# The first block's gates, queries, keys and values by seven block products in place of eight, with the sums of the weights made on VectorE

## The chip, the cores and the metric

The kernel runs on one NeuronCore of a Trainium2 chip. The metric is the device time of one execution in microseconds (us). The kernel before took 1728.72 us in the median of three runs (1728.32 to 1729.15).

## The reference

A token sequence of 512 tokens with 2048 features goes through two blocks; all values are float32. The change touches only the first, which puts 16 meta tokens in front (528 rows) and computes:

```python
hn = rmsnorm(h, pre_norm_g[layer])
proj = jnp.einsum('bld,dc->blc', hn, w_in[layer])
qa, ka, va, ga, qb, kb, vb, gb = jnp.split(proj, SPLIT_POINTS, axis=-1)
ya = gqa_axial_mixer(qa, ka, va, ...) * jax.nn.silu(ga)
yb = diff_attn_mixer(qb, kb, vb, ...) * jax.nn.silu(gb)
y = jnp.einsum('blc,cd->bld', jnp.concatenate([ya, yb], axis=-1), w_out[layer])
h = h + rmsnorm(y, post_norm_g[layer])
```

Mixer A has 8 query heads of 128 features on 2 key heads, mixer B has 8 heads with two softmaxes each. `ga`, `gb`, `qb`, `kb` and `vb` have 1024 columns each: 8 units of 128. The second block (stick-breaking attention, a convolution and a recurrence, another two projections) is left as it is.

## The kernel before, in words

**Products.** Each float32 operand is split into two float32r halves: `split` (L147 to L149) rounds to a high half on ScalarE (L148) and subtracts it on VectorE for the low half (L149). A product is then three matmuls, high x high, high x low, low x high (`PASSES`). The activations `big` hold both halves of all 16 K tiles (128 features each) of x, scaled by the norm's gain, 528 columns. The factor of the norm's root (`rbc`, one value for each token) is put in when a result is taken from PSUM.

**Weights.** The weights are packed on the host in half units of 128 x 1024 (eight K tiles of 128 columns). `load_next` loads a half unit on the SP queue (L266) into one of three buffers `wraw` and splits it into one of three buffers `wsp`. `take` asks for a half unit and lets two more be loaded ahead (`AHEAD`).

**Order of the first block.** KA, VA, QA0, then the eight gate units GA, QA1, the eight gate units GB, and for each of eight heads B the units QB, KB, VB; then the output projection O1. A gate or QB unit is 16 K tiles x 3 passes = 48 matmuls of 512 columns (`fm_real`), a KB or VB unit 96 matmuls of 264 columns (`fm_all`, 528 in two halves). A unit's result lies in a `pj` buffer of two PSUM banks, of which there are two. For a gate, `silu2` multiplies by `rbq` on VectorE (L432), takes the tanh on ScalarE (L433) and combines on VectorE (L434) into `ybuf`, where the attention's result is later multiplied in (`gate_y`, L439; for B L732). `split_y` then splits a slot of `ybuf` into `big` as the operand of O1.

**Who runs when.** The order on TensorE is written by a planner at build time: `run` takes steps of the main stream (the projections) and, when their due time by a clock of planned TensorE time has come, steps of side streams (the attention of each head: scores, softmax, transposes, values). So the matmuls of the heads stand between those of the projections, and on VectorE, ScalarE and the SP queue the instructions of both are mixed. Each engine takes its own instructions in that written order.

Of the kernel before, what the change touches and what calls it, by code (L numbers as in the profile page):

```python
# [16 lines left out]
P = 128  # L17
# [4 lines left out]
NM = 16  # L22
# [18 lines left out]

def _units():
# [6 lines left out]
    for name, n in (("KA", 2), ("VA", 2), ("GA", 8), ("QB", 8), ("KB", 8), ("VB", 8), ("GB", 8)):  # L49
        for i in range(n):  # L50
            u[(name, i)] = ("fm", 0, i, cols)
            cols += P
# [23 lines left out]

def _sequence():
# [19 lines left out]
def hybrid_two_block_kernel(ctx: ExitStack, tc: tile.TileContext, wp, xT, xtok, par, lvec, cst, rg, pg, lruw, out):  # L97
# [34 lines left out]
    def et(n=L):  # L132
        return T([P, L], "e", F32, 5)[:, :n]
# [98 lines left out]
    ybuf = T([P, KT, NTOK], "ybuf")  # L232
    yflat = flat(ybuf)
# [12 lines left out]
    h1d = dram.tile([NTOK, D], F32, tag="h1d", name="h1d")  # L246

# [7 lines left out]
    loaded = []  # L255

    def load_next(n=1024):
# [4 lines left out]
        raw = T([P, 1024], "wraw", F32, 3)  # L262
        w = T([P, 2, 1024], "wsp", F32R, 3)
# [7 lines left out]
    taken = [0]  # L271

    def take(unit, h):
        i = taken[0]
        assert seq[i] == (unit, h), (seq[i], unit, h)
        taken[0] = i + 1
        while len(loaded) < min(len(seq), i + 1 + AHEAD):
            for _ in load_next():
                pass
        return loaded[i]  # L280

# [15 lines left out]
    def fm_two(units, ps, lag):  # L297

        w = [None, None]
        for i in range(KT + lag):  # L300
            for u, kt in ((0, i), (1, i - lag)):
                if 0 <= kt < KT:
                    if kt % 8 == 0:
                        w[u] = take(units[u], kt // 8)
# [9 lines left out]
    def fm_all(unit, ps, after_kt=None):  # L314
        return fm(unit, [(ps[:, 0, :HL], (0, HL)), (ps[:, 1, :HL], (HL, L))], after_kt)

# [3 lines left out]
    def tm(units, x0, evac, kgs=range(4), toks=range(NT), before_unit=None, after_unit=None, chore=None):  # L320
# [4 lines left out]
        for i, unit in enumerate(units):  # L325
# [5 lines left out]
            if last:  # L331
                ws_ = [take(unit, 0), take(unit, 1)]
# [80 lines left out]
    kvraw = [ar[:, i * L : (i + 1) * L] for i in range(4)]  # L413
# [7 lines left out]
    qs_, ks_, vs_ = ar[:, 4608:5120], ar[:, 5120:5648], ar[:, 2560:3088]  # L421
    osb, osq, orr = ar[:, 3088:3600], ar[:, 3600:4112], ar[:, 1824:2336]
# [18 lines left out]
    def split_y(s):  # L441
        split(big[:, 0, s, :NTOK], big[:, 1, s, :NTOK], ybuf[:, s, :])

# [36 lines left out]
    def pv_steps(h, tag, e, cols, vt, vs, use, extra=()):  # L480

        for hf in range(2):
            yield when("pt", "ptt", (tag, h, 2 * hf))
            hold("pt")
            pt = T([P, 2, 4, 256], "pt", F32R)
# [37 lines left out]
    def side_norms():  # L523
# [3 lines left out]
        for j in range(5):  # L527
# [3 lines left out]
            xs = yflat[:n, (j % 2) * 2048 : (j % 2) * 2048 + 2048]  # L531
            nc.sync.dma_start(xs, xtok[j * P : j * P + n, :])
            act.activation(yflat[:n, 4096:6144], xs, AF.Square, accum_out=ss0[:n, j : j + 1])
# [24 lines left out]
    def side_kv(g):  # L558
# [3 lines left out]
        kb, t1, u = (yflat[:, (3 * g + i) * 640 : (3 * g + i + 1) * 640] for i in range(3))  # L562
# [71 lines left out]
    def a_sums(h, e):  # L634
        g = h // 4
        yield when(("gate", h), ("va", g))
        yield from pv_steps(h, "ea", e, lambda j: slice(j * P, min(L, (j + 1) * P)), lambda: va[g][0], lambda: va[g][1], lambda hf, o: gate_y(h, hf, o))
        post(("y", h), 1500)
# [4 lines left out]
    def b_values(h, vt):  # L643
        yield when(("projv", h), "pss", *([("sumb", h - 2)] if h > 1 else [("suma",)]))
        vt[:] = v_tiles(vs_, h % 2)
# [60 lines left out]
    def b_sums(h, e, vt):  # L706
# [6 lines left out]
        yield from pv_steps(h, "eb", e, tile_cols, lambda: vt[0], lambda: vt[1], use, [("normed", h - 1)] if h else [])  # L713
# [17 lines left out]
        y = ybuf[:, 8 + h, :]  # L731
        dve.tensor_tensor(y, osb, y, ALU.mult)  # L732
        post(("normed", h))
        post(("y", 8 + h), 5000)


    yt = blocks(yflat, D)
# [193 lines left out]
    def main_work():  # L931
# [4 lines left out]
        for i in range(2):  # L936
            ps = pjt()
            yield from fm_all(("VA", i), ps)
            act.copy(halves(kvraw[2 + i]), ps[:, :, :HL])
            post(("kv", 2 + i), 1000)  # L940

        def qa(c):
            def evac(accs):
                yield when("rbc", *([("qaused", 0)] if c else [("va", 0), ("va", 1)]))
                for t in accs:
                    act.mul(qraw[:, t, :], accs[t], rnat[:, t : t + 1])

            yield from tm([(f"QA{c}", kg) for kg in range(4)], NM, evac)
            post(("qa", c), 1000)

        def gate(unit, slot):
            ps = pjt()
            yield from fm_real(unit, ps, NM)
            ins = silu2(ps[:, 0, :], rbq, ybuf[:, slot, :])
            post(("gate", slot), 2000)
            return ins

        yield from qa(0)
        for h in range(8):
            yield from gate(("GA", h), h)  # L960
        yield from qa(1)
        for h in range(8):
            ins = yield from gate(("GB", h), 8 + h)
        with tc.issue_after(ins):
            lnload[0] = act.preload_act_table_set("natural_log_exp_and_others").ins

        def split_ready(kt):
            if there(("y", kt)) and kt not in ysplit:
                ysplit.add(kt)
                split_y(kt)  # L970

        def spread(kt):
            if kt % 4 == 3:
                split_ready(kt // 4)

        ysplit = set()
        for h in range(8):
            ps = pjt()
            yield from fm_real(("QB", h), ps, NM)
            if h:  # L980
                yield when(("qkused", h - 1))
            dve.scalar_tensor_tensor(qs_, ps[:, 0, :], -0.125, rbq, op0=ALU.mult, op1=ALU.mult)
            ps = pjt()
            yield from fm_all(("KB", h), ps)
            dve.tensor_tensor(halves(ks_), ps[:, :, :HL], halves(rbc), ALU.mult)
            post(("projb", h))
            ps = pjt()
# [257 lines left out]
```

## Time and profile before

| what | value |
|---|---|
| median of the runs | 1728.72 us |
| profiled execution | 1727.61 us |
| its span | 1725.8 us |
| busy share of TensorE (PE) | 99% |
| busy share of VectorE (DVE) | 59% |
| busy share of ScalarE (ACT) | 45% |
| granted TensorE clock | 1.00 |
| HBM read, written | 175.89 MB, 8.39 MB |

A page names engines PE (matmuls), PEld (weight loads), DVE (VectorE), ACT (ScalarE), POOL (GpSimd) and SP (the queue that issues DMAs). A group row has the line in the kernel, engine, operation, what is written <- what is read, shapes and count; then busy us and mean ns of one; then the idle time of the engine just before them and what ended it. A row in order of time has start, length, engine, line and tiles; a row that ends in x92 merges 92 instructions. Matmuls overlap, so their pace is read from starts.

### The profile page before, as it was taken

The page shows a single profiled execution, that of the slowest core. Times are in us where ns is not written, and L with a number is a line of the kernel's source. Part 1 is how long each engine was busy: PE and PEld are TensorE (multiplying, and loading weights), DVE is VectorE, ACT ScalarE, POOL GpSimd, SP SyncE. Part 2 cuts the span into 40 slices and gives each one's busy share as a digit, 9 for nine tenths or more (in the row PEclk, how much of TensorE's full clock was granted, in tenths as well). Part 3 has the DMA queues.
Part 4 walks back from the last instruction along what each step waited for, and adds up shares of the span by engine and source line. Part 5 has one row for each costly group of instructions (what it writes and reads, how often), then busy time and mean ns, then how long its engine had stood idle before and what let it go on. Part 6 is the DMA issues. An engine that isn't in the chain of part 4 may idle for free.

```text
span 1725.8 us, 23791 instructions
## 1 busy us (share of the span) xinstructions
PE 1714.7 (99%) x9496; PEld 1477.6 (86%) x9496; DVE 1015.9 (59%) x1694; ACT 783.8 (45%) x1276; POOL 91.0 (5%) x85
## 2 busy tenths in 40 slices
PE   8999999999999999999999999999999999999998
PEld 8888888889999999988788998888888888888887
DVE  5748634864566666775557869743223664575433
ACT  6434423443445555564445547822223664575311
POOL 0100001100001101000000001100000000010000
PEclk9999999999999999999999999999999999999999
DMA  8321122222221222222567653222222212432223
GB/s 314 121 98 62 63 84 86 68 79 74 76 84 64 72 74 74 74 69 78 171 196 270 218 190 109 92 94 90 98 98 90 81 61 88 153 115 74 86 97 123
DMA packets 53854, 185.81 MB, mean 108 GB/s; under 512 B 6112, under 2 KB 7776, under 8 KB 52064
## 3 DMA queue, kind: packets, MB, share of 16 engines
q1 hardware_dynamic: 53744, 184.30, 32.2%
q8 instruction: 74, 1.21, 0.3%
q14 instruction: 36, 0.29, 0.1%
HBM read 175.89 MB, written 8.39 MB: 107 GB/s over the span
## 4 chain that ended last, share of the span: by engine, by line
PE 96%; DVE 2%; issue 0%; DMA 0%; POOL 0%; ACT 0%; SPq 0%; DVEq 0%; ACTq 0%; POOLq 0%
PE pj L181 84%; PE pmt L181 4%; PE pss L181 4%; PE ptt L184 2%; PE pmt L184 1%; PE bank L181 1%; PE pss L184 1%; DVE wsp L149 0%; DMA wraw<-in_wp 0%; POOL ybuf L450 0%; SPq L374 0%; ACT wsp L148 0%; POOL ar L450 0%; SPq L266 0%; DVE sm L574 0%
## 5 line engine op out<-in xcount | busy, mean ns | idle before, releaser
L181 PE MATMUL pj<-big,wsp 128*128 128x264 f32 (+2 forms) x4608 | 809.0, 332 | 5.9 <-ACT big L375 5.3
L181 PEld LDWEIGHTS pj<-big,wsp 128*128 128x128 f32 x4608 | 688.2, 189 | 86.9 <-ACT big L375 5.6
L181 PE MATMUL pj<-wsp,big 128*128 128x512 f32 x3072 | 736.5, 396 | 0.6 <-DVE big L149 0.6
L181 PEld LDWEIGHTS pj<-wsp,big 128*128 128x128 f32 x3072 | 569.6, 188 | 131.3 <-DVE big L149 0.9
L149 DVE TENSOR_TENSOR wsp<-wraw,wsp 128x1024 fp32r<-128x1024 f32 (+1 forms) x299 | 363.1, 1215 | 387.1 <-ACT wsp L148 386.7
L148 ACT CAST wsp<-wraw 128x1024 fp32r<-128x1024 f32 (+1 forms) x299 | 310.8, 1040 | 496.0 <-PE pj L181 391.6
L148 ACT CAST pt<-ptt 128x512 fp32r<-128x512 f32 (+2 forms) x96 | 50.3, 524 | 76.1 <-PE ptt L184 76.1
L687 ACT ACTIVATE e<-e,sm 128x528 f32<-128x528 f32 x64 | 47.2, 737 | 77.6 <-DVE sm L684 77.1
L149 DVE TENSOR_TENSOR pt<-ptt,pt 128x512 fp32r<-128x512 f32 (+2 forms) x96 | 59.4, 619 | 35.4 <-ACT pt L148 34.7
L181 PEld LDWEIGHTS pmt<-pt,vv 128*128 128x128 f32 x528 | 69.1, 190 | 3.6
L181 PE MATMUL pss<-kk,qq 128*128 128x264 f32 x448 | 71.4, 287 | 0.0
L181 PE MATMUL pmt<-pt,vv 128*128 128x256 f32 (+1 forms) x528 | 69.6, 280 | 0.0
L181 PEld LDWEIGHTS pss<-kk,qq 128*128 128x128 f32 x448 | 63.5, 188 | 3.7
L684 DVE CUSTOM_DVE_ANT_0 e<-pss,ar 128x528 f32<-128x528 f32 x64 | 45.0, 703 | 31.4 <-PE pss L181 30.9
L184 PE MATMUL ptt<-ident,e 128*128 128x128 f32 x336 | 52.6, 273 | 0.1
L184 PEld LDWEIGHTS ptt<-ident,e 128*128 128x128 f32 x336 | 40.6, 140 | 6.9 <-DVE e L627 0.5
L432 DVE TENSOR_TENSOR e<-pj,rbc 128x512 f32<-128x512 f32 x32 | 22.0, 688 | 39.7 <-PE pj L181 39.7
L885 POOL TENSOR_SCALAR_AFFINE_SELECT e<-e 128x128 f32<-128x128 f32 x32 | 15.7, 490 | 476.2 <-ACT e L884 471.1
L654 POOL TENSOR_SCALAR ar<-ar 128x912 f32<-128x912 f32 x8 | 23.4, 2930 | 211.9 <-DVE sm L684 207.4
L624 ACT ACTIVATE e<-pss,sm 128x528 f32<-128x528 f32 x32 | 22.4, 701 | 23.5 <-DVE sm L622 23.4
L450 POOL TENSOR_TENSOR ar<-ar 128x256 f32<-128x256 f32 x16 | 18.4, 1172 | 242.9 <-DVE ar L447 242.9
L894 ACT ACTIVATE e<-e 128x128 f32<-128x128 f32 (+3 forms) x32 | 15.0, 470 | 28.8 <-DVE e L893 28.5
(202 smaller groups left out, 1168.9 us busy)
## 6 DMA issues: line engine op xcount, KB each, us to landing
wraw<-in_wp SPq DMA_DIRECT2D x295, 512.0 KB, 3.5
e<-in_xT SPq DMA_DIRECT2D x16, 264.0 KB, 4.4
ybuf<-in_xtok SPq DMA_DIRECT2D x4, 1024.0 KB, 7.2
ar<-in_xtok SPq DMA_DIRECT2D x4, 1024.0 KB, 5.9
h1d<-ybuf SPq DMA_DIRECT2D x4, 1024.0 KB, 5.4
ybuf<-h1d SPq DMA_DIRECT2D x12, 256.0 KB, 3.6
out<-ybuf SPq DMA_DIRECT2D x12, 256.0 KB, 2.1
ar<-in_pg SPq DMA_DIRECT2D x1, 1024.0 KB, 4.8
```

Source lines behind the costliest of these rows:

```text
L148: act.copy(hi, src)
L149: dve.tensor_tensor(lo, src, f(hi), ALU.subtract)
L181: _queue(nc.tensor.matmul(out, lhsT, rhs, start=start, stop=stop).ins, cost)
L184: _queue(nc.tensor.transpose(out, in_, identity).ins, 110.0)
L432: dve.tensor_tensor(g, g_ps, rb, ALU.mult)
L450: pool.tensor_tensor(v4(blocks(u))[:, :, :, a, :], v4(x)[:, :, :, 1 - a, :], v4(blocks(s))[:, :, :, a, :], ALU.mult)
L624: act.activation(halves(x), sv, AF.Exp, bias=nm, accum_out=l[:, 0:1])
L654: pool.tensor_scalar(bias, dist, 2.0 ** (-(h + 1)), None, op0=ALU.mult)
L684: dve.tensor_tensor_reduce(out=halves(x), in0=s[:, :, :HL], in1=halves(bias[:, b0 : b0 + L]), scale=1.0, scalar=3e38, op0=ALU.add, op1=ALU ...
L687: act.activation(x, x, AF.Exp, scale=-1.0, bias=nm, accum_out=l[:, m : m + 1])
L885: pool.affine_select(z[:, t * P : w], z[:, t * P : w], [[-1, P]], ALU.is_gt, -1e30, base=0, channel_multiplier=1)
L894: act.activation(c, c, AF.Exp)
```

## The change

Units are taken in 20 pairs (`PAIRS`): two gates, QB with KB of a head, or VB of two heads. Over the first 12 K tiles the pair is a 2 x 2 block product: two halves of the K tiles (`KS` = 6 each), two halves of the tokens (264 each), two units. Seven block products with sums of blocks replace the eight. The last four K tiles (`NCL` = 4) are computed as before, and added in PSUM (`rest`).

- The sums of the blocks of x are made once, by `side_x`, from x loaded again, into `x23`, `x1s` and over a part of `big`.
- The sums of the blocks of the weights are made for each pair on VectorE, by `produce`: four additions of 128 x 768. Seven splits of 768 columns and two of 512 replace four of 1024. Raw weights and split weights lie in four slots each in the same memory as before.
- `seven` runs the products of a pair on four PSUM banks, and combines them in eight VectorE operations on 264 (or 248) columns.
- The memory of `ybuf` is taken by `x23` in this stage. The gates are written to HBM (`gated`) and fetched when a head needs them; a head's result goes to HBM (`yd`) and is fetched for its split (`fetch_y`). All of these stand on the SP queue.
- QA1 moves ahead of the gates, and its result goes through HBM (`qd`); VA1 moves behind it. The pool of `e` buffers has six in place of five. In the last half of a unit one half unit less is asked for ahead, in the whole kernel. Weights of O1 are not loaded before the last pair (`barred`).

```diff
-    seq = [("VA", 0), ("VA", 1)] + [("QA0", kg) for kg in range(4)]
-    seq += [("GA", i) for i in range(8)] + [("QA1", kg) for kg in range(4)] + [("GB", i) for i in range(8)]
-    for h in range(8):
-        seq += [("QB", h), ("KB", h), ("VB", h)]
+    seq = [("VA", 0)] + [("QA0", kg) for kg in range(4)] + [("QA1", kg) for kg in range(4)] + [("VA", 1)]
...
-        return T([P, L], "e", F32, 5)[:, :n]
+        return T([P, L], "e", F32, 6)[:, :n]
...
+    def load_raw(p, r, slot):
...
+        nc.sync.dma_start(raw, wq[p, r] if r < 4 else wc[p, r - 4])
+    def produce(p, i):
...
+        add = lambda a, b: dve.tensor_tensor(r(a), r(a), r(b), ALU.add)
...
+        n = NCL * P if i in (6, 8) else WS
+        if i == 2:
+            add(0, 1)
+        slot = at[place]
+        w = halves(wsp_all[:, 2 * WS * slot : 2 * WS * slot + 2 * n])
+        pair_w[(p, i)] = w
+        split(w[:, 0], w[:, 1], r(src))
+        if i == 2:
+            add(0, 2)
+            add(1, 2)
+        elif i == 3:
+            add(0, 3)
...
+    def seven(p, r, c0a, c0b, evac_a1, evac_b, evac_a2, after=None):
...
+        yield from product(1, 0, lambda xs, j: big[:, xs, j, X1], allc, True, True)
+        produce(p, 5)
+        act.copy(p1s[:], r[0][:, :HL])
+        yield from product(3, 1, lambda xs, j: x23[:, xs, j, X1], allc, True, True)
+        produce(p, 6)
+        dve.tensor_tensor(wv[:], r[1][:, :HL], p1s[:], ALU.subtract)
+        yield from product(4, 2, lambda xs, j: x23[:, xs, j, X2], allc, True, True)
+        produce(p, 8)
+        dve.tensor_tensor(us[:], r[2][:, :HL], wv[:], ALU.add)
+        yield from product(5, 0, lambda xs, j: big[:, xs, KS + j, c0a:HL], slice(c0a, HL), True, False)
+        produce(p, 7)
+        yield from product(2, 1, lambda xs, j: x1s[:, xs, j, :], allc, True, True)
+        produce(p, 9)
+        dve.tensor_tensor(wv[:], r[1][:, :HL], wv[:], ALU.add)
+        dve.tensor_tensor(ts[:], r[1][:, :HL], us[:], ALU.add)
+        yield from rest(6, 0, 3, c0a, (False, True))
+        produce(p + 1, 1)
+        yield from evac_a1()
+        yield from rest(8, None, 2, 0, (False, True))
+        yield from product(7, 1, lambda xs, j: big[:, xs, j, HL + c0b : L], slice(c0b, HL), True, False)
+        produce(p + 1, 2)
...
+        yield from rest(8, 1, None, c0b, (False, False))
+        produce(p + 1, 3)
+        yield from evac_b()
+        yield from product(9, 3, lambda xs, j: big[:, xs, KS + j, X2], allc, False, True)
+        produce(p + 1, 4)
+        yield from evac_a2()
...
+    def side_x():
...
+            dve.tensor_tensor(b[:, HL:], a[:, HL:], b[:, HL:], ALU.subtract)
+            dve.tensor_tensor(a[:, HL:], a[:, HL:], a[:, :HL], ALU.subtract)
+            dve.tensor_tensor(a[:, :HL], a[:, :HL], b[:, HL:], ALU.subtract)
+            dve.tensor_tensor(s4raw[:, j], b[:, :HL], a[:, :HL], ALU.subtract)
+            split(x23[:, 0, j], x23[:, 1, j], a)
+            split(x1s[:, 0, j], x1s[:, 1, j], b[:, HL:])
...
+        split(big[:, 0, :KS, HL:], big[:, 1, :KS, HL:], s4raw.whole())
...
+        def use(hf, o):
+            y = ys[hf]
+            dve.scalar_tensor_tensor(y, o, 0.5, y, op0=ALU.mult, op1=ALU.mult)
+            nc.sync.dma_start(yd[h][:, hf * 256 : (hf + 1) * 256], y)
...
+            def silu(g, s):
+                th = et(NTOK)
+                last_tanh[0] = act.activation(th, g, AF.Tanh, scale=0.5).ins
+                dve.scalar_tensor_tensor(g, th, 1.0, g, op0=ALU.add, op1=ALU.mult)
+                nc.sync.dma_start(gated[s], g)
...
+            def evac_b():
+                g = et(NTOK)
+                dve.tensor_tensor(g[:, :HR], r1[:, NM:HL], wv[:, NM:], ALU.add)
+                dve.tensor_tensor(g[:, HR:], r2_[:, :HL], ts[:], ALU.add)
+                dve.tensor_tensor(g, g, rbq, ALU.mult)
+                silu(g, slot + 1)
```

**TensorE, the gates.** Where the gates GA begin, TensorE of the kernel before has (`pj` is the result in PSUM, `wsp` the split weights, `ar` holds a head's queries, `kk` and `qq` its keys and queries for the scores `pss`):

```order
L181 MATMUL pj<-big,wsp 128x512 x75
L184 MATMUL pmt<-ident,ar 128x128 x4
L181 MATMUL pj<-big,wsp 128x512 x19
L181 MATMUL pss<-kk,qq 128x264 x6
L181 MATMUL pj<-big,wsp 128x512 x20
```

The first pair of gates of the changed kernel stands there so (`x_1057` is `x23`):

```order
L196 MATMUL pj<-big,wsp 128x264 x15
L196 MATMUL pj<-x_1057,wsp 128x264 x36
L196 MATMUL pj<-big,wsp 128x248 x18
L196 MATMUL pj<-x1s,wsp 128x264 x18
L196 MATMUL pj<-big,wsp 128x248 x12
L196 MATMUL pj<-big,wsp 128x264 x24
L196 MATMUL pj<-big,wsp 128x248 x30
L196 MATMUL pj<-big,wsp 128x264 x36
```

The 512-column matmuls of two units (96) have become 174 of 264 and 248 columns; the last row holds the last product of this pair and the first of the next.

**VectorE, a gate.** One gate unit and its neighbours on VectorE of the kernel before (`wsp` the low half of a weight split, L432 and L434 the gate, the rest belongs to a head):

```order
L432 TENSOR_TENSOR e<-pj,rbc 128x512
L149 TENSOR_TENSOR wsp<-wraw,wsp 128x1024
L434 SCALAR_TENSOR_TENSOR ybuf<-e 128x512
L149 TENSOR_TENSOR pt<-ptt,pt 128x4x128
L502 TENSOR_TENSOR ptail<-pmt,ptail 16x256
```

About two thirds of the first gate pair on VectorE of the changed kernel (`xmisc` holds the combined products, L353 is a sum of weights):

```order
L164 TENSOR_TENSOR wsp<-wraw,wsp 128x512
L164 TENSOR_TENSOR wsp<-wraw,wsp 128x768
L462 TENSOR_TENSOR xmisc<-pj,xmisc 128x264
L463 TENSOR_TENSOR xmisc<-pj,xmisc 128x264
L164 TENSOR_TENSOR wsp<-wraw,wsp 128x768
L1217 TENSOR_TENSOR e<-pj,xmisc 128x248
L164 TENSOR_TENSOR wsp<-wraw,wsp 128x768
L1223 TENSOR_TENSOR e<-pj,xmisc 128x264
L353 TENSOR_TENSOR wraw<-wraw 128x768 x2
L164 TENSOR_TENSOR wsp<-wraw,wsp 128x768
L353 TENSOR_TENSOR wraw<-wraw 128x768
L1222 TENSOR_TENSOR e<-pj,xmisc 128x248
```

The combinations, sums and splits stand in one line; a split's low half waits for its high half on ScalarE, and a combination for its product.

**The SP queue, heads A.** Before, the queue from the tables of the first block to O1's gain is loads of weights, but for one table of B:

```order
L536 DMA ar<-in_cst 128x1280
L537 DMA ar<-in_rg 128x512
L266 DMA wraw<-in_wp 128x1024 x46
L653 DMA ar<-in_cst 128x912
L266 DMA wraw<-in_wp 128x1024 x66
```

Now, beside the gates GA (`wq` and `wc` are a pair's weights, `xmisc<-gated` is a fetched gate, `yd` a head's result):

```order
L345 DMA wraw<-in_wq 128x768 x4
L848 DMA yd<-xmisc 128x256
L843 DMA xmisc<-gated 128x256
L1212 DMA gated<-e 128x512
L345 DMA wraw<-in_wc 128x512
L848 DMA yd<-xmisc 128x256
```

A write of a head's result or of a gate waits for VectorE, and the weights behind it wait with it.

More of the change, by code (lines that the diff above doesn't have):

```diff
@@ L271, in hybrid_two_block_kernel, with take @@
     taken = [0]
-    def take(unit, h):
+    barred = [seq.index((("VA", 1), 1)) + 1]
+    def take(unit, h, ahead=AHEAD):
         i = taken[0]
@@ L965, in main_work @@
+        for name in ("GA", "GB"):
+            for i in range(0, 8, 2):
+                yield from gates(name, i)
+        with tc.issue_after(last_tanh[0]):
             lnload[0] = act.preload_act_table_set("natural_log_exp_and_others").ins
+        ysplit = set()
         def split_ready(kt):
```

322 lines of the change are left out of this document (259 added, 63 removed).

## The prediction

> **What bounds the kernel now.** I read the page's busy shares and its chain first, then the table of stages, then the paces on TensorE, then VectorE's groups and its order of time.
>
> ```profile
> span 1725.8 us, 23791 instructions
> PE 1714.7 (99%) x9496; PEld 1477.6 (86%) x9496; DVE 1015.9 (59%) x1694; ACT 783.8 (45%) x1276; POOL 91.0 (5%) x85
> PE 96%; DVE 2%; issue 0%; DMA 0%; POOL 0%; ACT 0%; SPq 0%; DVEq 0%; ACTq 0%; POOLq 0%
> ```
>
> TensorE is busy 99% of the span and is 96% of the chain: no other engine holds it up for long. The share of 59% for VectorE is a mean over stages, so I asked for the stages that the change rebuilds (columns: window, its length, busy us and count of PE, PEld, DVE, ACT, POOL, granted clock, DMA share, GB/s).
>
> ```profile
> 107.21:229.18 121.97, 121.92 (x662) 103.83 (x661) 86.36 (x176) 52.50 (x95) 9.21 (x8) 1.00 0.22 74
> 229.18:276.03 46.85, 46.85 (x212) 38.18 (x211) 11.33 (x13) 11.27 (x14) 0.00 (x0) 1.00 0.24 79
> 276.03:742.05 466.02, 465.99 (x3144) 428.76 (x3143) 312.89 (x585) 226.47 (x423) 40.13 (x23) 1.00 0.23 75
> ```
>
> The first row is the gates GA, the second QA1, the third the gates GB with queries, keys and values. Rows one and three together are the part that changes: 588.0 us, in which TensorE never rests and VectorE is already busy 86.4 + 312.9 = 399.3 us (68%), since the attention of the heads runs beside it. The headroom is 188.7 us on VectorE and nothing on TensorE.
>
> **TensorE: what is saved.** The pace is the distance of starts, not a matmul's mean duration, since matmuls overlap.
>
> ```profile
> 107.21 17.67 PE L181 MATMUL pj<-big,wsp 128*128 128x512 f32 x75
> 124.72 0.60 PE L184 MATMUL pmt<-ident,ar 128*128 128x128 f32 x4
> ...
> 451.35 4.80 PE L181 MATMUL pj<-big,wsp 128*128 128x264 f32 x38
> 455.99 0.66 PE L181 MATMUL pss<-kk,qq 128*128 128x264 f32 x4
> ...
> 468.37 1.60 PE L181 MATMUL pmt<-pt,vv 128*128 128x256 f32 x12
> 469.81 0.28 PE L181 MATMUL pmt<-ptail,vtail 96*128 96x256 f32 x1
> ...
> 1501.26 0.85 PE L181 MATMUL bank<-kk,qq 128*128 128x128 f32 x6
> 1501.95 1.33 PE L181 MATMUL pj<-wsp,big 128*128 128x512 f32 x5
> ```
>
> 512 columns take 17.51/75 = 0.2335 us, 264 take 4.64/38 = 0.1221, 256 take 1.44/12 = 0.120. In the last stretch three of six are 128 wide and three 256 (the program's sizes), 0.115 on average, so 128 columns still cost 0.110. The new width of 248 lies between 0.110 and 0.120; I take 0.117, next to the 256.
>
> A gate pair was 96 x 0.2335 = 22.42 us and becomes 114 x 0.1221 + 60 x 0.117 = 20.94. A query and key pair was 48 x 0.2335 + 96 x 0.1221 = 22.93 and becomes 144 x 0.1221 + 30 x 0.117 = 21.09. A value pair was 192 x 0.1221 = 23.44 and becomes 174 x 0.1221 = 21.25. With 8, 8 and 4 pairs the saving is 11.8 + 14.7 + 8.8 = 35.3 us (33 to 40 with the ends for 248). TensorE then asks for 588.0 - 35.3 = 552.7 us in the same work.
>
> **VectorE: what is added.**
>
> ```profile
> L149 DVE TENSOR_TENSOR wsp<-wraw,wsp 128x1024 fp32r<-128x1024 f32 x295 | 361.4, 1226 | 386.2 <-ACT wsp L148 385.8
> L432 DVE TENSOR_TENSOR e<-pj,rbc 128x512 f32<-128x512 f32 x32 | 22.0, 688 | 39.7 <-PE pj L181 39.7
> L434 DVE SCALAR_TENSOR_TENSOR ybuf<-e 128x512 f32<-128x512 f32 x32 | 21.8, 682 | 1.6 <-ACT e L433 1.6
> L149 DVE TENSOR_TENSOR big<-ybuf,big 128x512 fp32r<-128x512 f32 x32 | 21.2, 682 | 6.6 <-ACT big L148 6.5
> L439 DVE SCALAR_TENSOR_TENSOR ybuf<-pmt,ybuf 128x256 f32<-128x256 f32 x32 | 13.4, 417 | 11.4 <-PE pmt L181 11.4
> ```
>
> A two-tensor operation takes 0.682 us on 512 and 1.226 on 1024 columns, so 0.956 on 768; 264 columns out of PSUM take 0.42 (by the 256 row). Per pair the change takes away four splits of 1024 (4 x 1.226 = 4.90) and adds seven splits of 768 and two of 512 (8.06), four weight sums of 768 (3.82) and eight combinations of products (8 x 0.42 = 3.36). The scaling by the norm and the second step of the gate remain, from another source. Net 10.34 us per pair, for 20 pairs 206.8 us. VectorE would be busy 399.3 + 206.8 = 606.1 us where TensorE asks for 552.7: the bound moves to VectorE. This sum is my main reason; the next step is how tightly VectorE can pack.
>
> ```profile
> 213.22 1.23 DVE L149 TENSOR_TENSOR wsp<-wraw,wsp 128x1024 fp32r<-128x1024 f32 x1 [0.39 <-ACT wsp L148]
> 214.37 0.69 DVE L434 SCALAR_TENSOR_TENSOR ybuf<-e 128x512 f32<-128x512 f32 x1
> 214.97 0.42 DVE L439 SCALAR_TENSOR_TENSOR ybuf<-pmt,ybuf 128x256 f32<-128x256 f32 x1
> 215.30 0.68 DVE L149 TENSOR_TENSOR pt<-ptt,pt 128x512 fp32r<-128x512 f32 x1
> 215.90 0.70 DVE L622 TENSOR_REDUCE sm<-pss 128x1 f32<-128x528 f32 x1
> 217.46 0.16 DVE L626 RECIPROCAL sm<-sm 128x1 f32<-128x1 f32 x1 [0.86 <-ACT e L624]
> ...
> 740.00:760.00 20.00, 20.00 (x114) 17.13 (x113) 19.48 (x38) 13.38 (x27) 2.93 (x1) 1.00 0.24 79
> 140.00:180.00 40.00, 40.00 (x233) 34.76 (x232) 32.84 (x76) 18.18 (x37) 4.62 (x4) 1.00 0.20 66
> ```
>
> Where nothing is waited for, the next instruction starts 0.07 to 0.09 us before the last one ends (214.97 against 214.37 + 0.69). The change adds 20 x 21 - 80 = 340 instructions, worth about 25 us of overlap: 581 us is what VectorE needs if it never waits. [...]
>
> But it does wait: 0.86 us for ScalarE's exponential in a score tile, 0.39 for the high half of a split, and what stands behind in its order waits too. With work queued it reached 19.48 of 20 us (0.97); its 40 us in the attention of GA reached 0.82. I choose 0.94, nearer to the first, since now a queue will stand most of the time: 581/0.94 = 618 us, **30 us more** than the 588.0 of before.
>
> **The other parts.** ScalarE makes the high halves:
>
> ```profile
> L148 ACT CAST wsp<-wraw 128x1024 fp32r<-128x1024 f32 x295 | 309.2, 1048 | 494.6 <-PE pj L181 391.6 <-issue 85.1 <-DMA wraw<-in_wp 12.4
> L148 ACT CAST big<-ybuf 128x512 fp32r<-128x512 f32 x32 | 19.0, 616 | 13.3 <-PE pj L181 10.4 <-DVE ybuf L439 1.6 <-DVE ybuf L732 1.1
> ...
> wraw<-in_wp SPq DMA_DIRECT2D x295, 512.0 KB, 3.5
> h1d<-ybuf SPq DMA_DIRECT2D x4, 1024.0 KB, 5.4
> ybuf<-h1d SPq DMA_DIRECT2D x12, 256.0 KB, 3.6
> ```
>
> 20 x (7 x 0.83 + 2 x 0.62) - 80 x 1.048 = 57 us more, on 279 us in 553: no bound. The weights are the same bytes. Gates and outputs go out and come back in pieces of 128 or 256 KB, at the share of 0.22 of the DMA engines no matter for bandwidth; each trip costs about 3.6 us there and 3.6 back, hidden behind the transposes and products of the next half head, and 3.6 us each where that cover is short. On the SP queue the loads of weights now stand behind writes that wait for VectorE. A load lands 3.5 us after issue and is needed one to three products (2.2 us each) later, so a queue held for more than about 3 us shows on TensorE; I put this into the 0.94. Making the sums of x takes six steps of four operations of 264 (0.42), one of 528 (0.70) and one of 264, and at the end one of 1584 (1.8 by the same slope): 19 us of VectorE beside QA0, QA1 and VA1, where QA1 alone has 35 us free by the second stage row: 0 (up to 5 if late). At the hand-over to O1 no weights are loaded ahead: 3.5 for the load, 1.05 and 1.23 for the split, 5.8 at most; half of that lies under the last product, and with the trips of y through HBM I take 5 (0 to 10). The sixth buffer of e and the shorter look-ahead of a unit's last half cost nothing that I can find.
>
> Sum: the profiled execution took 1727.61 (span 1725.8; the median of the runs is 1728.72) + 30 + 5 = 1763, by the median 1764.
>
> **Rivals.** (a) *TensorE stays the bound* and the extra work of VectorE fits beside it. This needs VectorE to pack into 553 us, 28 less than my densest sum. For it: in the 20 us from 740 TensorE was busy for all 20.00 with VectorE at 19.48. Against: even without one wait the sum is 581. It decides if the 305 us of added rows come 9% cheaper than I took them. Time 1727.6 - 35.3 + 5 = 1697. Chance 0.12.
>
> (b) *VectorE bounds, but is always fed* (0.97 to 1.0): 581 to 599 us in place of 588.0, so 1721 with nothing lost at the hand-over and 1744 with 5 us lost: about no change. Chance 0.21.
>
> (c) *Lock-step.* TensorE stands at a transpose that waits for VectorE's scaled score, while VectorE's next instruction combines a product that is queued behind that transpose. Then VectorE is no denser than in the 40 us beside attention, 0.82: 581/0.82 = 709, 121 more, up to 1853; half way 1800. For it: four weight slots let weights be made only two or three products ahead, and with four banks product 2 overwrites product 3 as soon as VectorE has read it, two products (4.3 us) later. Against: independent splits and sums are mixed in between. Chance 0.21.
>
> (d) *A slow pace after rests.* The first microseconds of TensorE show it:
>
> ```profile
> 8.55:11.70 3.15, 3.15 (x16) 3.15 (x15) 2.46 (x4) 2.60 (x5) 0.00 (x0) 1.00 1.03 404
> 15.00:18.15 3.15, 3.15 (x29) 3.15 (x28) 1.82 (x3) 2.59 (x4) 0.00 (x0) 1.00 0.87 253
> ```
>
> 16 matmuls of 264 columns start in 3.15 us at first and 29 later, with the same granted clock of 1.00. If waits on VectorE send TensorE back to that pace for a third of the 421 us of products (20 pairs by the three sums above), they take 140 x (29/16 - 1) = 114 us more: 1877. It decides if single rests grow to microseconds; my picture has many short ones. [...] Chance 0.04.
>
> (e) *The change does not save what it says*, since 248 columns cost more than 256 or a matmul's weights load late: 720 x 0.1 us is 72 more. No row of that width exists. Chance 0.02.
>
> **Numbers.** My forecast has 0.40, the rest as above. Some 0.2% (3.5 us) is what a measurement of this kernel tells from no change. Faster: (a) and a third of (b), 0.19. Same: a third of (b), 0.07. Slower: the rest of (b), the forecast, (c), (d) and (e), 0.74. The forecast alone runs from 581/0.97 to 581/0.90, 1744 to 1791 with the hand-over. The range of 1712 to 1830 leaves out (a), (d) and the far part of (c), about 0.2.
>
> **What would show it.** Right: in the pairs' stage VectorE is above 90% busy, TensorE rests before products (idle of "pj" groups, released by VectorE's "wsp", or by a normalised e before transposes), the chain holds VectorE for tens of per cent there, and the stage has about 618 us; starts of 264 columns still stand 0.122 apart between rests, and those of 248 about 0.117. Wrong: TensorE still 99% busy there (then (a)), or VectorE under 85% with TensorE resting as well (then (c), or the SP queue if the rests end with "wraw").

## The result and the profile after

The changed kernel takes 1880.51 us (median of 4 runs, 1879.09 to 1883.93), the kernel before 1728.76 us beside it. The ratio is 1.0881, 95% interval 1.0862 to 1.09: slower by 151.8 us, against a forecast of 36 us slower and a range that ended at 1830.

The page of the profiled execution first: span, busy shares, the clock granted to TensorE in 40 slices, and the chain by engine. The chain's shares sum to 55% only, so I read the causes from the waits and not from it.

```profile
span 1882.0 us, 26415 instructions
PE 1734.9 (92%) x10288; PEld 1539.1 (82%) x10288; DVE 1212.0 (64%) x2071; ACT 859.7 (46%) x1421; POOL 85.4 (5%) x85
PEclk9999888899999989889989999999999999999999
PE 52%; DVE 1%; ACT 1%; DMA 1%; issue 0%; DVEq 0%; SPq 0%; ACTq 0%
```

TensorE went from 99% to 92% of a longer span, and VectorE, which I had expected to become the bound, is busy 64%. The table of stages says where. Its rows are the stage of the 20 pairs and all that follows (columns as before: window, length, busy us and count of PE, PEld, DVE, ACT, POOL, granted clock, DMA share, GB/s).

```profile
158.30:874.20 715.90, 599.93 (x4550) 585.46 (x4547) 547.84 (x1019) 322.69 (x606) 40.13 (x24) 0.93 0.26 80
874.20:1882.00 1007.80, 986.23 (x4905) 824.86 (x4904) 564.28 (x830) 457.14 (x700) 33.18 (x44) 0.99 0.38 122
```

The difference of the spans, 1882.0 - 1725.8 = 156.2 us, has three parts. The pairs begin at 158.30, where 107.21 + 46.85 = 154.06 us had gone by for the same work: 4.2 us. The stage has 715.9 us where it had 588.0: 127.9 us. What follows has 1007.8 where it had 1725.8 - 742.05 = 983.75: 24.1 us. In the stage TensorE rests for 715.9 - 599.9 = 116.0 us, and VectorE is busy for only 547.8/715.9 = 77%. Neither engine is the bound: they wait for each other. And TensorE's 599.9 us are 47 more than the 552.7 that it should ask for; the granted clock, 0.93, accounts for most of these: 599.9 x 0.93 = 558.

The groups tell what ends the rests (line, operation, count, busy us, mean ns, idle us before and who ended it).

```profile
L196 PE MATMUL pj<-big,wsp 128*128 128x264 f32 (+3 forms) x4320 | 657.3, 310 | 71.0 <-DVE xmisc L463 41.1 <-DVE ar L1284 8.1 <-ACT big L537 5.4
L196 PE MATMUL pj<-x,wsp 128*128 128x264 f32 x720 | 113.0, 317 | 47.2 <-ACT xmisc L451 44.4 <-issue 2.0 <-DVE ar L1263 0.7
L353 DVE TENSOR_TENSOR wraw<-wraw 128x768 f32<-128x768 f32 x80 | 76.8, 961 | 0.9
```

L451 is ScalarE's copy of product 1 out of bank 0, and the group that waits for it, `pj<-x`, holds product 3, which goes to bank 1. L463 reads product 2 out of bank 1, and what waits for it is the rest of product 6, which goes to bank 0. No data pass between these. The order of time shows one such wait, in the middle of a pair of queries and keys; TensorE has been idle since 775.96.

```profile
776.26 0.70 DVE L898 CUSTOM_DVE_ANT_0 e<-pss,ar 128x528 f32<-128x528 f32 x1
...
778.25 0.50 DVE L913 TENSOR_SCALAR e<-e,sm 128x528 f32<-128x528 f32 x1
778.67 0.95 DVE L164 TENSOR_TENSOR wsp<-wraw,wsp 128x768 fp32r<-128x768 f32 x1
779.53 0.76 DVE L914 SCALAR_TENSOR_TENSOR e<-e,sm 128x528 f32<-128x528 f32 x1
780.21 0.69 DVE L164 TENSOR_TENSOR pt<-ptt,pt 128x512 fp32r<-128x512 f32 x1
780.81 0.42 DVE L462 TENSOR_TENSOR xmisc<-pj,xmisc 128x264 f32<-128x264 f32 x1
781.15 0.95 DVE L164 TENSOR_TENSOR wsp<-wraw,wsp 128x768 fp32r<-128x768 f32 x1
782.02 0.43 DVE L463 TENSOR_TENSOR xmisc<-pj,xmisc 128x264 f32<-128x264 f32 x1
782.59 3.32 PE L196 MATMUL pj<-big,wsp 128*128 128x248 f32 x15 [6.63 <-DVE xmisc L463]
785.52 0.42 DVE L1254 TENSOR_TENSOR ar<-pj,xmisc 128x248 f32<-128x248 f32 x1 [3.07 <-PE pj L196]
```

The operation that TensorE waits for takes 0.43 us, but it stands in VectorE's queue behind a head's scores, three splits and one more combination: 5.8 us from 776.26 to 782.02, of which VectorE itself waits 0.90 for ScalarE in the rows left out. TensorE rests 6.63 us. Then VectorE rests 3.07 us for the next product. That is a lock-step as in rival (c), but at another place: there TensorE was to stand at a transpose, here it stands at a product, and the group of the transposes (`ptt<-ident,e`) has no idle time before it in this trace. Of the lead of two products that I had named, nothing is left.

**Theory A**: the four banks are two tiles of two banks each (`ta` and `tb`), and a product's wait goes by the tile: it waits for the last reader of either bank. Each product that follows a reading of the neighbour bank then starts only when VectorE or ScalarE has come round to that reading. **Theory B**, the rival: VectorE's added work (sums, combinations) sets the pace, whichever banks it reads.

### The profile page after: what moved, and what is told of

Same layout as the page of the kernel before. It is cut to its first block, busy times and chain, and to the rows that moved or that the text cites. A ratio compares the mean times of both kernels' runs of the same rounds, so it can differ in the third digit from the quotient of the medians.

```text
span 1882.0 us, 26415 instructions
## 1 busy us (share of the span) xinstructions
PE 1734.9 (92%) x10288; PEld 1539.1 (82%) x10288; DVE 1212.0 (64%) x2071; ACT 859.7 (46%) x1421; POOL 85.4 (5%) x85
## 3 DMA queue, kind: packets, MB, share of 16 engines
q1 hardware_dynamic: 73904, 206.43, 34.4%
## 4 chain that ended last, share of the span: by engine, by line
PE 52%; DVE 1%; ACT 1%; DMA 1%; issue 0%; DVEq 0%; SPq 0%; ACTq 0%
PE pj L196 47%; PE pmt L196 2%; PE pss L196 1%; PE bank L196 1%; PE ptt L199 1%; PE pss L199 0%; PE pmt L199 0%; DMA e<-yd 0%; DMA yd<-xmisc 0%; ACT wsp L163 0%; DVE big L164 0%; DVE pt L164 0%; ACT big L163 0%; ACT e L901 0%; ACT ptail L701 0%
## 5 line engine op out<-in xcount | busy, mean ns | idle before, releaser
L196 PE MATMUL pj<-wsp,big 128*128 128x512 f32 x3072 | 738.1, 397 | 12.6 <-ACT big L163 10.3
L196 PE MATMUL pj<-big,wsp 128*128 128x264 f32 (+3 forms) x4320 | 657.3, 310 | 71.0 <-DVE xmisc L463 41.1
L196 PEld LDWEIGHTS pj<-big,wsp 128*128 128x128 f32 x4320 | 599.2, 195 | 114.2 <-ACT wsp L163 20.1
L196 PEld LDWEIGHTS pj<-wsp,big 128*128 128x128 f32 x3072 | 571.5, 189 | 141.3 <-ACT big L163 10.7
L164 DVE TENSOR_TENSOR wsp<-wraw,wsp 128x1024 fp32r<-128x1024 f32 (+3 forms) x399 | 426.2, 1070 | 349.2 <-ACT wsp L163 338.4
L163 ACT CAST wsp<-wraw 128x1024 fp32r<-128x1024 f32 (+3 forms) x399 | 368.0, 924 | 545.1 <-PE pj L196 416.7
L196 PE MATMUL pj<-x,wsp 128*128 128x264 f32 x720 | 113.0, 317 | 47.2 <-ACT xmisc L451 44.4
L196 PEld LDWEIGHTS pj<-x,wsp 128*128 128x128 f32 x720 | 105.6, 218 | 52.1 <-ACT xmisc L451 48.7
L196 PE MATMUL pmt<-pt,vv 128*128 128x256 f32 (+1 forms) x528 | 74.1, 291 | 6.7 <-DVE ptail L702 5.1
L196 PEld LDWEIGHTS pmt<-pt,vv 128*128 128x128 f32 x528 | 71.6, 201 | 9.4 <-DVE ptail L702 3.7
L353 DVE TENSOR_TENSOR wraw<-wraw 128x768 f32<-128x768 f32 x80 | 76.8, 961 | 0.9
L196 PE MATMUL pss<-kk,qq 128*128 128x264 f32 x448 | 74.4, 295 | 0.2 <-DVE sm L898 0.2
L196 PEld LDWEIGHTS pss<-kk,qq 128*128 128x128 f32 x448 | 64.3, 196 | 2.4 <-DVE sm L898 0.8
L196 PE MATMUL pj<-x1s,wsp 128*128 128x264 f32 x360 | 49.4, 286 | 0.0
L196 PEld LDWEIGHTS pj<-x1s,wsp 128*128 128x128 f32 x360 | 45.8, 188 | 0.0
```

Of the source, the lines that this page charges most:

```text
L163: act.copy(hi, src)
L164: dve.tensor_tensor(lo, src, f(hi), ALU.subtract)
L196: _queue(nc.tensor.matmul(out, lhsT, rhs, start=start, stop=stop).ins, cost)
L353: add = lambda a, b: dve.tensor_tensor(r(a), r(a), r(b), ALU.add)
```

## The experiments

In e3 and e8 the line numbers are those of the changed kernel; elsewhere they are a few higher (L196 is L197 or L198).

**e1: four tiles of one bank.**

```
-        ta, tb = pjt(), pjt()
-        banks = (ta[:, 0], ta[:, 1], tb[:, 0], tb[:, 1])
+        banks = tuple(psq.tile([P, 512], F32, tag=f"pq{i}", name="pj") for i in range(4))
```

The pool of two-bank tiles is closed before the pairs and opened again after them.

> The changed kernel, with the pairs' four PSUM banks as four tiles of one bank in place of two tiles of two banks; the arithmetic is unchanged. Theory A (a wait goes by the tile: TensorE's next product into one bank of a tile waits for the reader of the other bank): TensorE's idle time before pj that L451 and L463 end (44.4 and 41.1 us after the change) nearly goes, the granted clock of the stage is 0.98 to 1.00, the pairs' stage falls from 716 us to 580 to 620, and the whole to 1740 to 1790 us. Theory B (VectorE's chain of sums, additions and evacuations sets the pace, whichever banks it reads): the stage stays above 690 us, the idle time moves to other lines of the pairs, and the whole is 1855 to 1885 us.

Measured: 1777.33 us, 103 below the after kernel and inside theory A's band; ratio to before 1.0282 (1.0267 to 1.0297). Groups, then the stage:

```profile
L197 PE MATMUL pj<-big,wsp 128*128 128x264 f32 (+3 forms) x4320 | 639.0, 305 | 11.3 <-ACT big L538 6.1 <-DVE wsp L165 2.6 <-ACT e L1163 1.4
L197 PE MATMUL pj<-x,wsp 128*128 128x264 f32 x720 | 100.4, 292 | 4.3 <-DVE wsp L165 3.7 <-ACT wsp L164 0.6
```

```profile
158.75:764.20 605.45, 565.18 (x4550) 555.91 (x4547) 539.08 (x1016) 317.14 (x600) 38.17 (x24) 0.98 0.31 94
```

The 85.5 us that L451 and L463 ended are gone, TensorE's rests in the stage fell from 116.0 to 40.3 us, its clock is 0.98. The arithmetic and VectorE's work are the same (539.1 against 547.8 us), so B as the cause of these 103 us has fallen. But VectorE now fills 89% of 605.5 us, so it may be the next bound. Since e1 also places the banks anew (`side="right"`), e8 keeps the two tiles and changes the grouping alone.

**e8: two tiles still, the banks grouped otherwise** (banks 0 and 2, 1 and 3), in the after kernel.

```
-        banks = (ta[:, 0], ta[:, 1], tb[:, 0], tb[:, 1])
+        banks = (ta[:, 0], tb[:, 0], ta[:, 1], tb[:, 1])
```

> The changed kernel, still with two tiles of two banks, but with banks 0 and 2 in one tile and 1 and 3 in the other. If a product waits for readers of the tile and not of the bank: product 3 (bank 1) no longer waits for L451, which reads bank 0, and product 7 no longer for the addition at L1217; product 5 (bank 0) now waits for the addition at L457, which reads bank 2 right behind product 4. The idle time that L451 ends (44.4 us) goes below 10 us, L457 ends 20 us or more, and the time is 1830 to 1870 us, between the two kernels. If waits go by the bank or VectorE's pace decides, the grouping changes nothing: 1875 to 1885 us, with L451 as before.

Measured: 1875.46 us. The groups:

```profile
L196 PE MATMUL pj<-big,wsp 128*128 128x264 f32 (+3 forms) x4320 | 672.8, 314 | 102.7 <-DVE xmisc L457 26.9 <-DVE e L1222 21.1 <-DVE ar L1257 13.3
L196 PE MATMUL pj<-x,wsp 128*128 128x264 f32 x720 | 101.2, 294 | 11.1 <-DVE ar L1263 4.2 <-DVE ar L1289 2.8 <-DVE wsp L164 2.1
```

The waits moved as theory A says: L451 ends 1.0 us where it ended 44.4, and L457, which reads bank 2, now ends 26.9 us before product 5, in bank 0 of the same tile. L1222 and L1257 read bank 1, and behind them product 9 goes to bank 3, now in the same tile: 34.4 us, where they had ended 4.4. The size I missed: the rests before the two groups are 113.8 us where they were 118.2, so the gain is 5 us and not 10 to 50. The other grouping, too, has neighbours that are still being read.

**e2, e3 and e11: the price of the weight sums**, left out with four tiles (e2) and with two (e3), and done twice with four tiles (e11).

```
-        add = lambda a, b: dve.tensor_tensor(r(a), r(a), r(b), ALU.add)
+        add = lambda a, b: None
```

```
+        def add(a, b):
+            for _ in range(2):
+                dve.tensor_tensor(r(a), r(a), r(b), ALU.add)
```

> The kernel with four tiles of one bank, and the 80 weight sums on VectorE (76.8 us) left out, so the products take unsummed weights. Theory A: VectorE has about 548 us of work in a stage of some 590, so it is nearly the bound once the banks are apart; without the sums it has 471 and TensorE is the bound: 1725 to 1740 us, 10 to 40 us below the kernel with the sums. Theory B: VectorE's work sets the pace in both, so leaving 77 us of it out brings 70 us or more.

> The changed kernel with its two tiles of two banks, and the 80 weight sums left out, so the products take unsummed weights. Theory A: the waits of the products on the readers of the other bank stay; only the queue ahead of those readers on VectorE is shorter: 10 to 50 us less, 1830 to 1870 us, and L451 still ends 30 us or more of TensorE's idle time. Theory B: 77 us of VectorE's work less is 70 us or more off the time, with the clock's share of the loss on top: below 1800 us.

> The kernel with four tiles of one bank, each weight sum done twice (80 more additions of 0.96 us, 76.8 us on VectorE; the products take weights to which the second block was added twice). Leaving the sums out brought 34.5 us of 76.8. If VectorE bounds the pairs from there on: 60 to 85 us more than 1777.3 us, 1837 to 1862 us. If the sums mostly fall into VectorE's rests and only their place in its queue costs: 20 to 45 us more, 1797 to 1822 us.

Measured: e2 1742.83 us (34.5 below e1, 3 above the end of theory A's band), e3 1837.99, e11 1847.80. The stage of e2, of e3 and of e11:

```profile
160.42:730.80 570.38, 555.56 (x4549) 551.45 (x4547) 472.84 (x937) 316.06 (x600) 38.75 (x24) 0.98 0.32 100
```

```profile
162.18:832.00 669.82, 582.51 (x4549) 569.80 (x4547) 479.23 (x938) 319.05 (x602) 39.25 (x24) 0.95 0.28 85
```

```profile
159.34:834.00 674.66, 583.51 (x4550) 566.71 (x4547) 608.81 (x1096) 318.35 (x602) 38.31 (x24) 0.95 0.28 85
```

With two tiles, taking 77 us from VectorE brings 42.5 us, and the stage is still 669.8 us at 72% of VectorE; L451 still ends 34.3 us of TensorE's rests and L463 40.2. With four tiles the three points make a curve: from 472.8 to 539.1 us of VectorE's work the stage grows by 35.1, from 539.1 to 608.8 by 69.2, one for one. So once the banks are apart, VectorE bounds the pairs from the amount of work in e1 upward, at a density of 539.1/605.5 = 0.89 and 608.8/674.7 = 0.90. Below that amount about half of what VectorE is spared reaches the stage (35.1 of 66.2 us), and without the sums TensorE is nearly the bound again, with 555.6 us of work, close to the 552.7 forecast. Theory B holds behind theory A, from there on.

**e4: the last head's result handed over directly**, on top of e1.

```
-        y = et(NTOK)
-        nc.sync.dma_start(y, yd[s])
+        if s == 15:
+            y = gin[:, :NTOK]
+        else:
+            y = et(NTOK)
+            nc.sync.dma_start(y, yd[s])
...
-        nc.sync.dma_start(yd[8 + h], y)
+        if h < 7:
+            nc.sync.dma_start(yd[8 + h], y)
...
-        post(("y", 8 + h), 7500)
+        post(("y", 8 + h), 7500 if h < 7 else 2500)
```

The last line tells the planner that this result is ready sooner.

> The kernel with four tiles of one bank, and the last head's gated result (slot 15) handed to the output projection straight from its tile in SBUF, without the write to HBM and the read back (3.83 and 2.60 us in the chain at the hand-over, with the time between them). If that trip is what TensorE waits for at the hand-over (10.3 us before big, L163): 4 to 9 us below the kernel with the trip. If the last head's attention itself is late, with other work behind it: within 2 us of it.

In the after kernel's chain the trip stood bare between the head's last step and the first products of the projection that need it:

```profile
976.68 0.70 DVE xmisc L952
977.39 0.02 issue
977.40 3.83 DMA yd<-xmisc
981.24 0.02 SPq L609
981.26 0.03 issue
981.29 2.60 DMA e<-yd
983.89 0.02 issue
983.91 0.63 ACT big L163
984.54 0.04 issue
984.59 5.79 PE pj L196 x12
```

Measured: 1772.53 us, 4.8 below e1, inside the first band. The part after the pairs is 1003.5 us, against 1011.1.

**e5: queries and keys of head 7 before the values of 6 and 7**, on top of e4.

```
-        pairs += [(("QB", h), ("KB", h)), (("VB", h), ("VB", h + 1)), (("QB", h + 1), ("KB", h + 1))]
+        trio = [(("QB", h), ("KB", h)), (("VB", h), ("VB", h + 1)), (("QB", h + 1), ("KB", h + 1))]
+        pairs += trio if h < 6 else [trio[0], trio[2], trio[1]]
...
             yield from qkb(h)
-            yield from vvb(h)
+            if h < 6:
+                yield from vvb(h)
             yield from qkb(h + 1)
+            if h == 6:
+                yield from vvb(h)
```

> The kernel with four tiles of one bank and the last head's result handed over directly, with the last two pairs of products exchanged: queries and keys of head 7 come before the values of heads 6 and 7, as they did before the change. Of the 20 us by which the part after the pairs is still longer than before the change (1003.5 against 983.8 us), most comes between the 200th and the 400th product of the output projection, where it waits for head 7. If head 7's late queries are the cause: 10 to 20 us less, 1752 to 1763 us, and the wait is gone. If it is the trips of gates and results through HBM and the splits that follow them: 3 us less at most, 1769 to 1774 us.

Measured: 1778.9 us, 6.4 above e4: both readings missed. The stage and what follows:

```profile
161.18:783.10 621.92, 575.54 (x4576) 564.84 (x4573) 549.08 (x1038) 324.06 (x615) 39.95 (x25) 0.96 0.29 91
783.10:1778.50 995.40, 983.03 (x4881) 821.94 (x4879) 557.07 (x810) 452.54 (x692) 32.04 (x43) 0.99 0.39 123
```

Against e4, what follows the pairs did fall, by 8.1 us, but the stage grew by 16.3. VectorE has 549.1 us of work there in place of 538.7: I take it that head 7's scores moved into a stage where VectorE has no room for them.

**e6, e10, e12: sums by adding transfers.** GpSimd issues transfers that add the second weights in SBUF: all 80 (e6, on e5, with the first sum of a pair issued one split earlier), the one sum in four that only product 4 takes (e10, on e4), and that sum simply left out (e12).

```
-        add = lambda a, b: dve.tensor_tensor(r(a), r(a), r(b), ALU.add)
+        add = lambda a, b: pool.dma_start(r(a), wq[p, b], accum_op=ALU.add)
```

In e10 it is one line, which e12 drops:

```
-            add(1, 2)
+            pool.dma_start(r(1), wq[p, 2], accum_op=ALU.add)
```

> The same kernel, order exchanged, with the 80 weight sums taken from VectorE: GpSimd issues transfers that add the second weights to the first in SBUF. Leaving the sums out brought 34.5 us once the banks were apart. If VectorE's work is what bounds the pairs then, and the transfers keep up: 20 to 35 us below the kernel with VectorE's sums, 1720 to 1740 us. If these transfers are late, or slow VectorE down: no gain, or a loss, with TensorE waiting before the products that take summed weights.

> The kernel with four tiles of one bank and the last head's result handed over directly, with one of the four weight sums of each pair (of the two weight blocks that only product 4 takes) made by an adding transfer that GpSimd issues; the other three stay on VectorE. All four as transfers were a chain of 5 us each, which TensorE waited for; this one has two products of time and nothing behind it. If VectorE's work bounds the pairs: 20 sums of 0.96 us less, 10 to 19 us below 1772.5 us. If GpSimd's issuing slows VectorE or the transfer is late: 1772 us or more.

> The kernel with one sum of four made by an adding transfer, without that transfer: product 4 takes an unsummed block, and no adding transfer is issued. It tells why the transfer brought nothing (1776.2 against 1772.5 us). If the transfer itself costs (late, or slowing VectorE and the other transfers): 1758 to 1766 us, a quarter of the 34.5 us that leaving out all sums brought. If this sum was free on VectorE: 1770 to 1777 us.

Measured: 1879.37 us (100 above e5), 1776.21 and 1765.46. In e6 an adding transfer lands 5.0 us after its issue, three of a pair stand in a row on the same block with a split between each two, and TensorE waits for the splits (waits of TensorE: us in total, times, longest):

```profile
wraw<-in_wq POOLq DMA_DIRECT2D x80, 384.0 KB, 5.0
```

```profile
PE pj L198 <- ACT wsp L165: 58.2, 19, 7.4
```

In e12 the missing sum brought 7.1 us on e4's 1772.53, near a quarter of e2's 34.5; e10, which makes it by transfer, lost 3.7. So 20 transfers that stand in no chain still cost 10.7 us together. VectorE is not slowed by them: a split takes 1072 ns on average in e10 and 1070 in e12, a weight sum 953 and 952. TensorE's rests for splits of weights are 8.9 us in e10 and 5.4 in e12, so some of the transfers are late; the rest of the 10.7 us stays open.

**e9 and e13: seven products for the gates alone** (e9, on e4; queries, keys and values by eight as before), and the same without its 32 sums (e13).

```
-        pairs += [(("QB", h), ("KB", h)), (("VB", h), ("VB", h + 1)), (("QB", h + 1), ("KB", h + 1))]
...
+            yield from fm_real(("QB", h), ps, NM)
...
+            yield from fm_all(("KB", h), ps)
...
+            yield from fm_all(("VB", h), ps, spread if h == 7 else None)
```

Behind the last gate pair, e9 and e13 also split the second half of the tokens again and go back to the two-bank tiles.

> Four tiles of one bank, seven block products for the gates alone (8 of 20 pairs); queries, keys and values by eight as before the change, with the second half of the tokens split again for K tiles 0 to 5 behind the last gate pair, since the pairs had put a combination there. TensorE saves 8 of 20 parts of 35.3 us: 14 us. VectorE gets 8 times 10.3 us in place of 20 times, so it has some 480 us in a stage of 575 (84%). If VectorE's load is what costs the rest once the banks are apart: 1720 to 1738 us. If it is the trips through HBM, the later start and the hand-over: 1745 us or more.

> The kernel with seven products for the gates alone, without its 32 weight sums (30.7 us on VectorE; the products take unsummed weights). That kernel loses all of its time before the end of the gates (428.3 against 398.1 us before the change; the rest is 1327 us in both). If VectorE's queue holds TensorE up there: 12 to 25 us less, 1730 to 1744 us. If it is the switch, the second splits of the tokens and the later start: 1750 us or more.

Measured: e9 1755.63 us (1.0158, 1.0143 to 1.0173), e13 1738.36. The pairs' stage of e9 and of e13:

```profile
156.50:428.20 271.70, 242.41 (x1953) 237.69 (x1951) 230.79 (x449) 129.38 (x243) 13.12 (x13) 0.97 0.32 101
```

```profile
160.42:409.10 248.68, 234.46 (x1945) 232.68 (x1942) 199.91 (x412) 123.22 (x237) 13.47 (x13) 0.98 0.36 110
```

From the first product behind the gates to the end, e9 takes 1327.1 us and the kernel before 1327.7 (e9, then before):

```profile
428.30:1755.40 1327.10, 1321.72 (x7341) 1143.26 (x7341) 773.49 (x1206) 617.81 (x1000) 58.25 (x55) 1.00 0.36 115
398.10:1725.80 1327.70, 1322.74 (x7348) 1141.96 (x7346) 774.08 (x1207) 618.65 (x1003) 62.05 (x55) 1.00 0.33 108
```

The whole loss lies ahead: these products start at 428.3 us, and at 398.1 before. So, with the last head handed over directly, the trips of gates and results through HBM cost nothing behind the gates where the order there is the old one. That points to the end of the pairs, and not to the trips, for most of the 24 us that the after kernel loses behind them. My 1720 to 1738 for e9 was wrong (the time lies in the other band, though not by its trips), because 84% was a mean over a stage in which VectorE has uneven work. Before the change the gates took 122.0 + 122.1 = 244.0 us, and with 11.8 saved TensorE would ask for 232; beside the attention of the heads A, VectorE alone has 230.8 us of work there. So neither had room, TensorE rests 29.3 of 271.7 us, and without the sums (e13) the stage is 23 us shorter and the time inside the first band. One rest of TensorE in both runs belongs to the experiment's own way back to the old order, at its first product behind the gates; in e9:

```profile
PE pj L197 <- DVE e L1237: 6.1, 1, 6.1
```

L1237 is the last combination of the last gate pair. It stands behind the repeated splits of the tokens, and the first product of the two-bank tiles waits for it, 6.1 us in e9 and 6.6 in e13. Ten microseconds above before remain in e13; a later start of the pairs (160.4 against 154.1) is six, and this rest is more than the other four.

No version with seven products beat the kernel before. The one that comes nearest with all its arithmetic is e9. The versions without any sum (e2, e13) stay above it too, so in these two a better place for the sums alone would not have turned the sign. No run combines this with a cheaper way back.

## Why the prediction was wrong

The direction was right, the size not: 1880.5 against 1764 and a range to 1830.

- *TensorE saves 35.3 us*: right as far as the traces show. Starts of 264 columns stand 0.122 us apart in the after kernel, of 248 columns 0.115 (median over the trace, 0.117 taken; so rival (e) has fallen), and with waits out of the way (e2) TensorE needs 555.6 us.
- *VectorE's added rows, 10.34 us per pair, 206.8 in all*: right. The durations of all its instructions rose by 226.7 us in sum, of which the sums of x have 18.9 (19 forecast); that leaves 10.39 per pair. A weight sum took 0.961 us (0.956 taken), a combination of 264 columns 0.42 to 0.43 (0.42). Counted without overlaps, its busy time rose from 1015.9 to 1212.0, 196.1 us.
- *VectorE needs 581 us in the stage*: 33 too many. It has 547.8 there, mainly because part of the attention no longer lies in the stage: behind the pairs VectorE is busy 16.4 us more than before, and ahead of them some 12 us more beyond the sums of x.
- *VectorE becomes the bound and packs to 0.94, 618 us*: this is the step that failed. TensorE and VectorE alternated, VectorE at 0.77 in 715.9 us, since a product waited for the readers of both banks of a tile (L451 and L463 ended 85.5 us of TensorE's rests). With four tiles of one bank (e1) VectorE packs to 0.89, the stage is 605.5 us and the time 1777, 13 from the forecast. The forecast is for the kernel that I had in mind, one whose banks are free one by one, and its nearness to e1 is in part luck: the need was less than forecast, the packing looser, and the 12 us by which the stage is shorter than 618 are more than lost behind it (27.4 us where I had put 5).
- *Rival (c), lock-step, 0.21*: the two engines did wait for each other, but not as (c) tells it. It has TensorE stand at a transpose that waits for a scaled score; the traces have it at products, behind readings of the neighbour bank. That its far end (709 us of stage, 1853) came near is luck in part: 581/0.82 stands against 547.8/0.77. One sentence of its support shows the error: "with four banks product 2 overwrites product 3 as soon as VectorE has read it, two products (4.3 us) later". The code says `pjt()` twice, two tiles of two banks, and e1 and e8 show that the tile is what a product waited for (the 85.5 us gone in e1, 26.9 us moved to L457 in e8). With a lead of two products I held the far part unlikely and left it out of the range.
- *Rival (d), half pace after rests, 0.04*: it came along with the lock-step, as a cost of its rests and not as a rival of its own: 47 us, not 114 (the 599.9 us of TensorE against 552.7). I misread its first row: the granted clock of 1.00 from 8.55 to 11.70 is no reading, since the clock's record in that trace begins at 11.76 us. Behind the long rests of the after kernel the record does show 0.50.
- *The hand-over and the trips, 5 us*: the part behind the pairs lost 24.1 us. There TensorE rests 21.6 us (5.0 before) and is busy 7.4 more. The last head's trip has 4.8 (e4). Some of the rest is attention that the pairs left behind: 38 matmuls more than before, and the 16.4 us on VectorE. e5 could move it, not remove it; what remains stays open.
- *Start of the pairs, 0 (up to 5)*: 4.2 us.
- The signs I had given: VectorE under 85% with TensorE resting was to mean (c) or the SP queue, and the rests ended with L451 and L463, not with `wraw`. As a sign of lock-step it held; it did not tell where.

## What to carry to other kernels

Ask of every buffer that is written in turns what the unit is that a writer waits for, the tile or the part of it that it touches: two banks in one tile were one buffer here (116.0 us of rests of TensorE in the stage, 40.3 with a tile for each bank), and the lead that I had counted in banks was not there. When a change moves work to an engine, count how much stands ahead of the operation that releases the other engine (5.8 us ahead of one of 0.43 us on VectorE here), and not only the busy sum; the mean of a stage hides the part of it that is already full. A version in which only the tiling is corrected (103 us here) tells whether the cost of a change is in its arithmetic or in its buffers.

## What the runs showed of the hardware

A long rest of TensorE cost twice in the after kernel, by itself and by the slower matmuls behind it. This is the timeline of TensorE in the after kernel behind a rest of 4.79 us, and the granted clock over these matmuls and those behind the rest of 6.63 us:

```profile
227.95 2.35 PE L196 MATMUL pj<-x,wsp 128*128 128x264 f32 x9 [4.79 <-ACT xmisc L451]
230.10 2.68 PE L196 MATMUL pmt<-pt,vv 128*128 128x256 f32 x12
```

```profile
227.90:230.10 2.20, 2.15 (x10) 2.15 (x11) 1.98 (x4) 0.63 (x1) 0.00 (x0) 0.50 0.31 119
782.50:785.70 3.20, 3.11 (x15) 3.14 (x16) 0.18 (x1) 0.00 (x0) 0.00 (x0) 0.53 0.36 123
```

Nine matmuls in 230.10 - 227.95 = 2.15 us are 0.24 each, about twice the usual 0.122. Over the stage of the pairs, the products behind rests of 1 to 2 us mostly go on at 0.12 (one, behind 1.93 us, at 0.22). Those behind 4 us or more go on at 0.22 or slightly less (8 rests) for 3 to 6 us, and those between 2 and 4 us at either. The trace's record of the granted clock has 21 stretches of 0.50 in this stage, 11 of 3.41 us and 10 of 6.83, and all their starts lie whole multiples of 3.41 us apart; so the loss came in such steps and was not in proportion to the rest. Eight rests from 1.9 to 3.2 us were followed by half pace too, so here a rest shorter than 4 us could be enough. As an estimate from these paces, a rest of 1 us cost 1 us here, and one of 5 some 7.
